# Second block: two prefetched weight units split behind the norm's rows, and another pace of expert loads

## The chip, the cores and the metric

The kernel runs on one core of one Trainium2 chip. The metric is the device time of one execution in microseconds (us); the kernel before has a median of 1340.48 us over 3 runs (1337.61 to 1340.64). A core has a matrix engine (PE, with its weight loads PEld), a vector engine (DVE), a scalar engine (ACT), GpSimd (POOL) and a sync engine (SP). In this kernel SP's queue issues all transfers from HBM that are named below.

## The reference, cut to what matters

The program is two layers of a first block (gated attention, a gated linear attention and a spatial gating unit, merged and normalised) and then a second block with a router and 32 experts. Here is where the change lies: the end of the first block's last layer, and the second block.

```python
out = merge(y_attn, y_gla, y_sgu, m_a, m_g, m_s)            # m @ w_out
x = layer_norm(ALPHA * x + gate * out, post_g, post_b)      # 256 rows of 1024
# second block
z = rmsnorm(x, mix_norm) @ w_in_2           # 2568 columns: q, k, v, forget, gate, recurrent input
att = forgetting_attention(q, k, v, log_f)
lru_out = rg_lru(conv(rec_in)) * gelu(gate_in)
x = x + concat([att, lru_out]) @ w_out_2
h2 = rmsnorm(x, ffn_norm)
y = experts(h2)                             # each token's two experts; w_gate, w_up, w_down: 3 MB an expert
out = rmsnorm(x + y, final_norm)
```

## The kernel before, in words

All matrix products of the dense parts are made of float32 values split in two: a weight *unit* (512 rows of 256 columns, 512 KB) is loaded into a tile `raw`, ACT copies it to a rounded high part (`split`, line 97), DVE subtracts that to a low part (line 98), and PE makes three products (high by high, high by low, low by high). The function `unit` issues the load on SP and the split behind it. The tiles `raw` rotate among three buffers, so the load of a unit waits until the split of the third unit before it is done.

`out_proj` (line 1040) is the last product of the first block. In the last layer it takes its 1024 columns in three steps: 512 columns (four units), 256 and 256 (two units each). After each step DVE scales the product by the gate (`ot`, line 1057), adds it to `x` (line 1058) and takes statistics (`bnst`, line 1060). Then `layer_norm` normalises both row tiles, and `make_hT` (line 493) turns the rows: PE transposes (`trh`), ACT and DVE write the high rows `h2Th` and the modulated rows `hmod`, and DVE subtracts them to the low rows `h2Tl` (line 516). The last ACT and DVE instructions of that stand in `self.last_h`.

Four units of `w_in_2` (its recurrent columns) are prefetched during `out_proj`. They are written into tiles named `ew`, which lie where the first block's rows lay; below they are E0 to E3. `self.pending` is a list of functions, and `tick(n)` calls the next n of them: two after the first step of `out_proj`, one after each of the others. Once the rows are there, the product `p2ps` (lines 1214 and 247) takes E0 and E1, and then E2 and E3. Meanwhile POOL and DVE apply the norm's weights to one row tile each (`x<-x,post`, lines 1198 and 1199), ACT squares the rows (line 1201), and a small product `rmps` (line 1208) spreads the two inverse norms over the partitions.

`second_dense` (line 1333) then projects: the forget columns `f` (two units), the gate columns `g` (four), `q` (four), `k` (four) and `v` (four wide units), 18 units in all. It computes the recurrence (`lru`) beside them. Then come the router's small loads (`router_setup`), the attention over two row tiles, and the output product with eight units of `w_out_2`.

The experts' weights are loaded ahead, in slots of 1 MB, by `load_step` (line 114): each call loads the next half of an expert's gate and up weights (`gu`) or its down weights (`dn`). Ten slots are open from the second block's start, three more once the recurrence's tiles are closed (line 1389), five after the dense part, and four in the experts' part. `paced_load` (line 190) counts the units of the whole program and calls `load_step` behind each second one, if there are slots. Up to the second block 162 units are counted. Behind `v` six calls of `load_step` stand together (line 1392); one without a free slot does nothing.

The order of the instructions on each engine's queue is set by a planner, which simulates a timeline and takes the instructions that it holds to be ready, those that are traced earlier first. `issue_after(ins)` puts what is traced under it behind `ins`, where both are on one engine. Each queue is then run in order on the chip.

Of the kernel before, what the change touches and what calls it, by code (L numbers as in the profile page):

```python
# [75 lines left out]
class Builder:  # L76
    def __init__(self, ctx, tc, a):
        self.ctx, self.tc, self.nc, self.a = ctx, tc, tc.nc, a
        self.after, self.last_tr = (), []
        self.n_split, self.share, self.n_lo = 0, 0, 0  # L80
        self.pending = []
        self.n_unit, self.n_load, self.loaded, self.expert_pools = 0, 0, {}, []
        self.ids, self.last_dn = {}, []
        self.n_bank, self.alternate, self.early = 0, False, {}
        self.nraw, self.nhi = 3, 3
# [104 lines left out]
    def paced_load(self, dma):  # L190

        self.n_unit += 1
        if self.expert_pools and self.n_unit % 2 == 0:
            with self.tc.issue_after(dma.ins):
                self.load_step()

# [871 lines left out]
    def first_block(self):  # L1068
        nc, tc, a = self.nc, self.tc, self.a
        with ExitStack() as st:  # L1070
# [92 lines left out]
            with ExitStack() as layer:  # L1163
                self.slot = self.pool("slot1", bufs=2, stack=layer, reuse_waits="tile")
                self.nhalf = 4
                self.layer_pools(layer)
                m2 = self.second_modulation()
                self.lru_const = self.second_setup(lruc)
                self.branches(((0, 256), (256, 512)))
                with ExitStack() as inner:  # L1170
                    self.merge_pools(inner)
                    h2p = self.pool("h2T", side="right", stack=self.right, reuse_waits="tile")
                    self.h2T = [h2p.tile([128, 8, 256], F32R, name=n) for n in ("h2Th", "h2Tl")]
                    pv = self.post_norm(0)
                    for t in range(2):
                        nc.gpsimd.tensor_tensor(x2[:, t], x2[:, t], pv[:, 0], op=OP.mult)
                        nc.gpsimd.tensor_tensor(x2[:, t], x2[:, t], pv[:, 1], op=OP.add)
                    pv = self.post_norm(1)
                    side = self.pool("lru", side="right", stack=self.right, reuse_waits="tile")
                    self.merge(iter(()))  # L1180

                    early = []

                    def early_unit(u):
                        if u % 2 == 0:
                            t = hp.tile([128, 4, 4, 256], F32R, tag="hTh" if u < 2 else "hTl", name="ew")
                            early.extend([(t[:, 0], t[:, 1]), (t[:, 2], t[:, 3])])
                        c0 = 2056 + 256 * (u // 2)
                        self.unit(a["w_in_2"][0][512 * (u % 2):512 * (u % 2) + 512, c0:c0 + 256], 256, early[u])

                    self.pending.extend([lambda u=u: early_unit(u) for u in range(4)])
                    self.out_proj([x2[:, 0], x2[:, 1]], self.gates(), ((0, 1),),
                                  lambda tts: self.make_hT([x2[:, 0], x2[:, 1]], tts, *m2, dst=self.h2T))
                    junk = self.mg.tile([128, D], F32, tag="gate", bufs=2, name="junk")
                    for tt in range(2):
                        eng = nc.vector if tt else nc.gpsimd
                        with tc.issue_after(self.last_h[1]):
                            eng.tensor_tensor(x2[:, tt], x2[:, tt], pv[:, 0], op=OP.mult)
                            eng.tensor_tensor(x2[:, tt], x2[:, tt], pv[:, 1], op=OP.add)
                        ms = self.sm.tile([128, 1], F32, tag="rms", name="rms")  # L1200
                        nc.scalar.activation(junk, x2[:, tt], AF.Square, scale=1.0 / 32, accum_out=ms)
                        self.rsqrt(self.rs2[:, tt:tt + 1], ms)
                    self.hTh, self.hTl = self.h2T

                    R = self.R = side.tile([128, 256], F32, name="rms2")
                    ps = self.psc.tile([128, 512], F32, tag="sc", name="rmps")
                    for tt in range(2):
                        nc.tensor.matmul(ps[:, tt * 128:tt * 128 + 128], self.rs2[:, tt:tt + 1].to_broadcast([128, 128]),
                                         self.ident, start=True, stop=True, skip_group_check=True)
                    nc.scalar.activation(R, ps[:, :256], AF.Copy)  # L1210
                    rT = self.rT = side.tile([128, 4, 259], F32, name="r2T")
                    nc.gpsimd.memset(rT[:, :, 0:3], 0.0)
                    for c in range(2):
                        for j, ps in enumerate(self.gemm_T(early[2 * c:2 * c + 2], 0, 256, "p2ps")):
                            nc.scalar.activation(rT[:, 2 * c + j, 3:259], ps, AF.Copy)
                    for c in range(4):
                        nc.vector.tensor_tensor(rT[:, c, 3:259], rT[:, c, 3:259], R, op=OP.mult)
# [115 lines left out]
    def second_dense(self, st):  # L1333
# [31 lines left out]
        u = self.chunk(w, 1536, 128)  # L1365
# [25 lines left out]
        self.hTr = big.tile([128, 8, 2, 128], F32, name="hTr")  # L1391
        for _ in range(6):
            self.load_step()

        yh[0], yl[0] = (big.tile([128, 4, 256], F32R, tag="ya", bufs=2, name="ya" + n) for n in "hl")
        for tt in range(2):
# [618 lines left out]
```

## Time and profile before

| what | value |
|---|---|
| median of 3 runs | 1340.48 us |
| profiled execution | 1342.97 us |
| its span, first to last instruction | 1341.1 us |
| PE busy | 1253.8 us (93%) |
| DVE busy | 716.0 us (53%) |
| ACT busy | 578.4 us (43%) |
| POOL busy | 350.6 us (26%) |
| mean granted PE clock, as a share of full speed | 0.976 |
| read from HBM | 241.27 MB |

The profile is of one execution, whose own time is 2.49 us over the median. Times in rows are microseconds from the span's start. A busy PE is not PE at its peak, since the ends of matmuls are modelled; how densely they start tells more.

### The profile page before, as it was taken

What the parts mean: (1) busy time and instruction counts of PE and PEld (TensorE: products, weight loads), DVE (VectorE), ACT (ScalarE), POOL (GpSimd) and SP (SyncE); (2) the same over time, 40 slices, a digit from 0 to 9 for tenths busy, and PEclk for the clock granted to TensorE, in tenths of its full rate; (3) what the DMA queues carried; (4) which work ended last, traced back from release to release, by engine and by line L of the source; (5) the groups of instructions that cost most, each with busy time, mean ns of one, the idle gap of its engine ahead of it and who ended that gap; (6) DMA issues with size and microseconds to landing.
All of it is one profiled execution on the core that took longest, in us unless ns stands there. A gap on an engine that the chain in (4) does not pass through costs nothing. (4 is left out here: it accounts for less than half of the span.)

```text
span 1341.1 us, 21494 instructions
## 1 busy us (share of the span) xinstructions
PE 1253.8 (93%) x8099; PEld 934.1 (70%) x8099; DVE 716.0 (53%) x1412; ACT 578.4 (43%) x1099; POOL 350.6 (26%) x373
## 2 busy tenths in 40 slices
PE   5999999999999999999999989999799989999975
PEld 3679778777777666789887878799698685333221
DVE  2546585675553223368778777655787555111102
ACT  2463453535433222346776554544466434222201
POOL 2327743630000101143367455001054020000000
PEclk8999999999999999999999999999899989999988
DMA  9523232211114577545555435246469556999994
GB/s 309 187 64 100 78 90 69 64 47 54 58 48 120 182 240 229 175 157 157 160 165 156 136 96 188 79 118 179 145 243 331 167 200 256 410 409 408 409 409 180
DMA packets 169873, 243.81 MB, mean 182 GB/s; under 512 B 15285, under 2 KB 130205, under 8 KB 169761
## 3 DMA queue, kind: packets, MB, share of 16 engines
q1 hardware_dynamic: 169760, 242.35, 53.7%
q8 instruction: 66, 1.08, 0.3%
q14 instruction: 47, 0.38, 0.1%
HBM read 241.27 MB, written 1.05 MB: 181 GB/s over the span
## 5 line engine op out<-in xcount | busy, mean ns | idle before, releaser
L98 DVE TENSOR_TENSOR wlo<-raw,whi 128x1024 fp32r<-128x1024 f32 (+1 forms) x202 | 251.6, 1250 | 153.0 <-ACT whi L97 151.4
L97 ACT ACTIVATE whi<-raw 128x1024 fp32r<-128x1024 f32 (+1 forms) x216 | 212.6, 993 | 197.5 <-PE mgps L248 35.1
L247 PE MATMUL mgps<-hTh,whi 128*128 128x512 f32 (+1 forms) x384 | 133.6, 349 | 4.9 <-DVE msum L991 2.6
L249 PE MATMUL mgps<-hTh,wlo 128*128 128x512 f32 (+1 forms) x384 | 132.0, 347 | 0.1
L248 PE MATMUL mgps<-hTl,whi 128*128 128x512 f32 (+1 forms) x384 | 131.7, 343 | 0.0
L994 POOL TENSOR_TENSOR msum<-msum,tanh 128x512 f32<-128x512 f32 (+1 forms) x32 | 35.2, 1104 | 343.6 <-DVE tanh L993 325.9
L1781 PE MATMUL gups<-gu,xw 128*64 128x512 f32 (+1 forms) x512 | 100.2, 618 | 6.4 <-DMA gu<-w_up 6.4
L247 PEld LDWEIGHTS mgps<-hTh,whi 128*128 128x128 f32 x384 | 73.4, 192 | 19.6 <-issue 6.2
L249 PEld LDWEIGHTS mgps<-hTh,wlo 128*128 128x128 f32 x384 | 73.3, 191 | 11.7 <-issue 3.6
L248 PEld LDWEIGHTS mgps<-hTl,whi 128*128 128x128 f32 x384 | 73.6, 192 | 9.0 <-issue 1.9
L1781 PEld LDWEIGHTS gups<-gu,xw 128*64 128x64 f32 (+1 forms) x512 | 25.3, 124 | 60.7 <-issue 58.9
L298 PE MATMUL gmt<-whi,hTh 128*128 128x512 f32 x160 | 61.2, 398 | 2.6 <-ACT qs L639 1.3
L299 PE MATMUL gmt<-wlo,hTh 128*128 128x512 f32 x160 | 62.8, 393 | 0.3 <-DVE wlo L98 0.2
L222 POOL TENSOR_TENSOR frs<-rsq,mhalf 128x1 f32<-128x1 f32 x2 | 1.1, 547 | 235.3 <-DVE frs L1955 235.3
L300 PE MATMUL gmt<-whi,hTl 128*128 128x512 f32 x160 | 62.5, 391 | 0.0
L1813 DVE SCALAR_TENSOR_TENSOR eth<-eth,gups 128x256 f32<-128x256 f32 x12 | 5.1, 421 | 102.3 <-ACT eth L1812 102.3
L1836 PE MATMUL dnps<-dn,hm 128*64 128x512 f32 (+1 forms) x256 | 51.4, 610 | 5.1 <-DMA dn<-w_down 5.1
L651 DVE TENSOR_REDUCE ast<-asc 128x1 f32<-128x512 f32 (+1 forms) x48 | 28.6, 600 | 42.2 <-PE asc L646 42.1
L661 ACT ACTIVATE pt<-trp 128x512 f32<-128x512 f32 (+1 forms) x48 | 24.9, 526 | 56.2 <-PE trp L659 50.7
L283 PE MATMUL gmt<-wlo,hTh 128*128 128x256 f32 x160 | 45.7, 286 | 1.8 <-DVE wlo L98 1.8
L98 DVE TENSOR_TENSOR ol<-dnps,oh 128x512 fp32r<-128x512 f32 x24 | 16.6, 690 | 57.2 <-ACT oh L97 57.2
L282 PE MATMUL gmt<-whi,hTh 128*128 128x256 f32 x160 | 45.4, 284 | 0.6 <-ACT g L742 0.6
(571 smaller groups left out, 3282.4 us busy)
## 6 DMA issues: line engine op xcount, KB each, us to landing
raw<-w_in SPq DMA_DIRECT2D x132, 512.0 KB
gu<-w_gate SPq DMA_DIRECT2D x64, 512.0 KB
gu<-w_up SPq DMA_DIRECT2D x64, 512.0 KB
dn<-w_down SPq DMA_DIRECT2D x28, 1024.0 KB
adar<-w_ada SPq DMA_DIRECT2D x32, 512.0 KB
raw<-w_out SPq DMA_DIRECT2D x32, 512.0 KB
adaw<-w_ada SPq DMA_DIRECT2D x16, 512.0 KB
raw<-w_in SPq DMA_DIRECT2D x32, 256.0 KB
```

What stands on the lines that cost most here:

```text
L97: nc.scalar.activation(hi, x, AF.Copy)
L98: return (eng or nc.vector).tensor_tensor(lo, x, hi.bitcast(F32), op=OP.subtract).ins
L247: nc.tensor.matmul(ps, wh, xh, start=(u == 0 and k == 0), stop=False)
L248: nc.tensor.matmul(ps, wh, xl, start=False, stop=False)
L249: nc.tensor.matmul(ps, wl, xh, start=False, stop=(u == len(acts) - 1 and k == 3))
L282: nc.tensor.matmul(out[tt], xh, hi[:, j, :n], start=first, stop=False, skip_group_check=True)
L283: nc.tensor.matmul(out[tt], xh, lo[:, j, :n], start=False, stop=False, skip_group_check=True)
L298: nc.tensor.matmul(out[tt], xh, hi[:, j], start=(i == 0 and j == 0), stop=False)
L299: nc.tensor.matmul(out[tt], xh, lo[:, j], start=False, stop=False)
L300: nc.tensor.matmul(out[tt], xl, hi[:, j], start=False, stop=(i == 3 and j == 1))
L1781: mm = nc.tensor.matmul(u["ps"][pr], u["x"][:, k, pr], u["gu"][ei][k // 4][:, :, k % 4], start=(k == 0), stop=(k == 7), skip_group_check=T ...
L1836: mm = nc.tensor.matmul(ps[pr], hm[:, f, pr], dns[ei][:, f, 512 * hf:512 * hf + 512], start=(f == 0), stop=(f == 1), skip_group_check=True ...
```

## The change: what it does

Of the four prefetched units only E0 and E1 are left in `pending`, so `out_proj` calls both after its first step. E2 and E3 are called after `out_proj`, with `self.after` set to `last_h`: their splits stand behind the last ACT and the last DVE instruction of the norm's rows. Their loads are traced there too, behind the last units of `out_proj`.

The count in `paced_load` is compared with a new `pace`, which is 3, so that an expert's load follows each third unit; behind the six calls it becomes 1, so that each of the eight units of `w_out_2` calls for a load.

```diff
@@ __init__
+        self.pace = 3
@@ paced_load
-        if self.expert_pools and self.n_unit % 2 == 0:
+        if self.expert_pools and self.n_unit % self.pace == 0:
             with self.tc.issue_after(dma.ins):
                 self.load_step()
@@ first_block
-                    self.pending.extend([lambda u=u: early_unit(u) for u in range(4)])
+                    self.pending.extend([lambda u=u: early_unit(u) for u in range(2)])
                     self.out_proj([x2[:, 0], x2[:, 1]], self.gates(), ((0, 1),),
                                   lambda tts: self.make_hT([x2[:, 0], x2[:, 1]], tts, *m2, dst=self.h2T))
+
+                    self.after = self.last_h
+                    for u in (2, 3):
+                        early_unit(u)
+                    self.after = ()
@@ second_dense
         for _ in range(6):
             self.load_step()
+        self.pace = 1
```

## Rows read from the trace of the kernel before

**Rows 1.** Busy us by stretch: from, to, length, engines (instructions), clock, DMA.

```profile
core 0: us, PE busy (x) PEld busy (x) DVE busy (x) ACT busy (x) POOL busy (x), PEclk, DMA share, GB/s
947.50:960.50 13.00, 12.08 (x97) 11.50 (x95) 10.50 (x17) 5.31 (x5) 0.00 (x0) 1.00 0.75 226
...
966.10:985.20 19.10, 16.89 (x112) 15.93 (x112) 14.31 (x21) 9.46 (x17) 5.79 (x3) 0.81 0.15 45
985.20:1021.40 36.20, 36.13 (x286) 35.14 (x286) 30.09 (x47) 26.21 (x42) 16.14 (x9) 1.00 0.99 353
1021.40:1030.90 9.50, 7.48 (x50) 7.33 (x49) 5.91 (x6) 5.20 (x7) 6.13 (x3) 0.82 0.70 261
1030.90:1074.00 43.10, 41.08 (x240) 30.41 (x239) 26.54 (x53) 22.02 (x56) 3.64 (x4) 1.00 0.68 213
...
1130.00:1310.00 180.00, 166.50 (x840) 56.21 (x836) 31.08 (x86) 37.23 (x105) 0.00 (x0) 0.97 1.03 408
```

**Rows 2.** SP's queue during `out_proj`: start, time, line, transfer, count.

```profile
945.05 0.37 SPq L109 DMA_DIRECT2D raw<-w_in  x1
947.67 2.65 SPq L109 DMA_DIRECT2D raw<-w_out  x2
952.28 2.23 SPq L109 DMA_DIRECT2D raw<-w_in  x4
```

**Rows 3.** ACT at the end of `out_proj`; brackets: idle before, and what ended it.

```profile
958.16 1.06 ACT L97 ACTIVATE ew<-raw 128x1024 fp32r<-128x1024 f32 x1 [2.73 <-DMA raw<-w_in]
```

**Rows 4.** DVE at the end of `out_proj`, three of its rows.

```profile
956.61 0.75 DVE L1057 TENSOR_TENSOR ot<-gmt,gate 128x256 f32<-128x256 f32 x2
959.25 1.23 DVE L98 TENSOR_TENSOR ew<-raw,ew 128x1024 fp32r<-128x1024 f32 x1 [1.89 <-ACT ew L97]
...
963.96 0.26 DVE L934 BATCH_NORM_AGGREGATE bnmv<-bnst 128x2 f32<-128x24 f32 x1
```

**Rows 5.** PE: a gap in the last step of `out_proj`, and the first transposes.

```profile
954.70 0.39 PE L283 MATMUL gmt<-wlo,mm 128*128 128x256 f32 x1 [0.87 <-DVE wlo L98]
...
966.13 1.97 PE L505 MATMUL trh<-ident,x 128*128 128x128 f32 x8 [5.65 <-ACT x L942]
```

**Rows 6.** DVE behind the norm's rows.

```profile
976.38 0.69 DVE L516 TENSOR_TENSOR h2Tl<-hmod,h2Th 128x512 fp32r<-128x512 f32 x1
977.00 3.42 DVE L1198 TENSOR_TENSOR x<-x,post 128x1024 f32<-128x1024 f32 x1
...
982.96 1.21 DVE L1199 TENSOR_TENSOR x<-x,post 128x1024 f32<-128x1024 f32 x1
```

**Rows 7.** POOL beside the norm's rows.

```profile
974.02 2.41 POOL L1198 TENSOR_TENSOR x<-x,post 128x1024 f32<-128x1024 f32 x1 [8.88 <-issue]
976.51 2.83 POOL L1199 TENSOR_TENSOR x<-x,post 128x1024 f32<-128x1024 f32 x1
```

**Rows 8.** PE: the last prefetched product, the norms, and a later pause.

```profile
984.20 0.28 PE L249 MATMUL p2ps<-h2Th,ew 128*128 128x256 f32 x1
985.23 0.49 PE L1208 MATMUL rmps<-ident,rs 128*128 128x128 f32 x2 [0.75 <-POOL rs L222]
...
1023.44 0.39 PE L247 MATMUL p2ps<-h2Th,whi 128*128 128x256 f32 x1 [2.02 <-ACT qk2T L1330]
```

**Rows 9.** SP's queue ahead of the attention.

```profile
1026.40 1.18 SPq L133 DMA_DIRECT2D dn<-w_down  x2
1030.70 6.79 SPq L109 DMA_DIRECT2D raw<-w_out  x2
```

**Rows 10.** ACT: the first split of a unit of `w_out_2`.

```profile
1040.15 1.06 ACT L97 ACTIVATE whi<-raw 128x1024 fp32r<-128x1024 f32 x1 [0.44 <-DMA raw<-w_out]
```

**Rows 11.** PE: that unit's first product, and the transpose of two loaded rows.

```profile
1046.81 0.39 PE L282 MATMUL gmt<-whi,y2h 128*128 128x256 f32 x1
...
1049.84 0.23 PE L1531 MATMUL trf<-ident,fnrow 16*128 16x16 f32 x1
```

**Rows 12.** POOL: a copy that waits for one of the router's small loads.

```profile
1048.86 0.30 POOL L1524 CAST before<-braw 128x128 fp32r<-128x128 f32 x1 [13.52 <-DMA braw<-k_f]
```

## The prediction

> **What bounds the kernel now.** I read the busy times by stretch first, then the queues of each engine around the norm, then those ahead of the attention.
>
> Busy times by stretch [rows 1]: from 1130 to 1310 us the transfers are full (share 1.03, 408 GB/s). That is the experts' part, and it ends when the remaining bytes have come. Its slots come free when the dense part and the router are done, so a microsecond won or lost ahead of it moves the end by one. From 985.2 to 1074 the bound is PE: 36.13 of 36.2 us, with 286 matmuls, which is 0.126 us each, and later 41.08 of 43.1. The transfers are full as well up to 1021 (0.99), but PE does not wait for them. Two stretches in between are not full. In 966.1 to 985.2 PE starts only 112 matmuls, at a mean clock of 0.81, and in 1021.4 to 1030.9 only 50, at 0.82: the clock is partly at its lower level (1.2 instead of 2.4 GHz) after pauses of 5.65 and 2.02 us [rows 5, 8].
>
> The pause of 5.65 us is the norm's. PE ends the last step of `out_proj` at 966.13 - 5.65 = 960.48 and starts the transposes at 966.13 [rows 5]. In between DVE is the late one: it idles 1.89 us, does E3's subtraction (1.23 us, from 959.25), and has the statistics of both row tiles behind that, up to 963.96 + 0.26 = 964.22 [rows 4]. It idles for E3's copy on ACT, which waited 2.73 us for E3's load [rows 3]. That load was issued at 952.28, when E2's split had given its buffer back [rows 2].
>
> **First part: E2 and E3 behind the rows.** What goes from DVE ahead of the statistics is 1.89 us of idle time and two subtractions of about 1.2 us [rows 4], 4.3 us. Not all of it is won, as PE is next. E2's load at 945.05 took a buffer that the first unit of `out_proj`'s last step gets now; it can be issued there instead of at 947.67 [rows 2], 2.6 us sooner, and the gap of 0.87 us in which PE waited for its split [rows 5] goes. So PE ends at 959.6. Behind it DVE has three small instructions of the second row tile (0.75 / 2 = 0.38 us each [rows 4]) and the aggregate of 0.26: 961.0 instead of 964.22, 3.2 us sooner. The inverse norm, the normalisation and the transposes follow as before, so the last `h2Tl` ends at 973.9 instead of 977.07, and POOL starts its pair, which waits for the last transposes, at 970.8 instead of 974.02 [rows 6, 7].
>
> What comes back: on ACT two copies of 1.06 us [rows 3] behind its last row. ACT is busy for 9.46 of 19.1 us there [rows 1], and that hides them; without this cover they would cost their 2.1 us in front of the copies out of the product's bank. On DVE two subtractions, 2.4 us, behind the last `h2Tl`. Queued behind them are `x` (L1198 and L1199), whose end lets ACT square the rows, and then the inverse norm, for which PE waits with `rmps` at 985.23, 0.75 us idle [rows 6, 8]. In the order of before this chain gains 3.2 - 2.4 = 0.8 us. If the planner puts L1199 further ahead (before, it stands some 2.5 us behind the end of L1198, at 980.42), up to 3.2. I see no way below nothing: the two subtractions are the same ones that stood ahead of the norm.
>
> PE does not spoil this. The second half of the prefetched product, 48 matmuls, takes 48 x 0.126 = 6.0 us from E2's low part on. If that is done at 973.9 + 1.2 = 975.1, the product ends at 981.1; if it stands behind POOL first, as L1198 did, 2.3 us later, at 983.4. Before it ended at 984.20 + 0.28 = 984.48 [rows 8], so it gains 1.1 to 3.4 us, the same range. I take 2.0 us for this part, midway between 0.8 and 3.2, since the planner's order is in no row.
>
> L1198 on DVE took 3.42 us and L1199, of the same shape, 1.21. POOL's second instruction ran until 976.51 + 2.83 = 979.34, and L1198 ended 1.08 us behind that [rows 6, 7]: it stood still meanwhile. The Trainium skill (SBUF — State Buffer, "Who interferes with whom") says that a DVE instruction with two inputs in SBUF and a GpSimd instruction that reads SBUF hold a shared port for a whole instruction, and the other is blocked. By it the moved subtractions fall into POOL's pair, and the work of both engines adds up whoever is first: this part would be worth the 0.8. If the two engines ran side by side there, it would be worth some 3.1.
>
> **Second part: the pace of the loads.** Of the 18 units of the second block's projections nine were followed by a load, and six are now, since 162 units are counted ahead of them. They stand behind the 3rd, 6th, 9th, 12th, 15th and 18th. So 3 MB less run beside the projections up to about 1026 us. That is worth nothing by itself, since PE is full there [rows 1]: shorter landings make room only where nobody waits. Its worth has two bounds: nothing, and the whole of the later pause, which is 9.5 - 50 x 0.126 = 3.2 us with the time at the lower clock [rows 1, 8]. That pause ended with a copy on ACT and not with a load, so I take nothing.
>
> The three loads come back behind `v`. Before, two `dn` loads stood there at 1026.40 [rows 9]; now the one behind the 18th unit and four of the six calls follow each other, and with the load behind the 15th unit ahead of the pause, the net is 2 MB more in front of the first unit of `w_out_2`, issued at 1030.70 [rows 9]. At 408 GB/s [rows 1] these take 5.1 us. That unit's copy on ACT started at 1040.15, ended by its load [rows 10]; now 1045.3, less the 2.0 us won, 1043.3. With 1.06 and 1.23 us for its split it is ready at 1045.6. PE wants it at 1046.81 - 2.0 = 1044.8 [rows 11]: 0.8 us late. The router's small loads stand behind it in the queue. One landed at 1048.86 [rows 12], and PE transposes a later one at 1049.84 [rows 11], so at most 1.0 us of room is left there. SP itself is not late: the issue of five loads takes some 4 us, and it waits for a buffer until 1030.70 anyway. I take 0.5 us for this part, since DVE and ACT have idle time ahead of that split, with bounds of 0 and 5.1. The load after the first unit of `w_out_2` is one of three that need the later slots and costs nothing: from 1030.9 to 1074 the transfers are busy for 0.68 [rows 1].
>
> **The sum.** -2.0 + 0.5 = -1.5 us. The profiled execution took 1342.97 us (span 1341.1), so it would take 1341.5; the median of the runs is 2.5 us below it, and I expect 1340.48 - 1.5 = 1339.0 us.
>
> **The rivals.** (1) Faster: the norm's 3.2 us all arrive, and the lighter transfers let the planner order ACT so that the pause at 1021.4 goes, 3.2 more: 1334.1. For it speaks that the pause is one of order on ACT and that both stretches get other neighbours; against it, that nothing in the change touches the recurrence on which ACT waits.
> (2) Slower: the loads massed behind `v` decide, at the first product of `w_out_2` and the small rows behind it. From about 2.3 us of lateness that nothing covers PE stands still as at 1021.4, and the clock falls: 5.1 us, and 9.5 - 6.3 - 2.0 = 1.2 for the lower clock, less the 2.0 won, is +4.3: 1344.8. For it speaks the room of 1.0 us at most; against it, ACT's and DVE's idle time.
> (3) The change does not do what it says: the planner moves other splits or the expert loads into the places left, and the norm starts no sooner. Then 1340.5.
>
> **How the numbers follow.** Forecast 0.45, faster rival 0.32, slower rival 0.17, the third 0.06. A measurement of this kernel can tell about 0.3% from no change, that is 4.0 us: below 1336.5 and above 1344.5. So faster 0.33, within 0.50 (the forecast and the third, less 0.01), slower 0.17. The range reaches from 1332.5 to 1346.0: both rivals' times, each with about half of the runs' own spread of 3.0 us. The forecast's own range is 1336.5 to 1341.5.
>
> **What would show it.** Right: the first transposes at about 962.9 and the last `h2Tl` at 973.9; two `ew` subtractions behind it on DVE, one of them long; `rmps` at about 983.2; six `gu` loads up to 1026 us and four in a row behind `v`; PE as full as before up to 1074. Wrong: a pause of PE over 2 us before the products of `w_out_2` or the transpose of the small rows (the slower rival), no pause at 1021 (the faster one), or a norm that starts no sooner.

## The result, and the profile after

The change makes the kernel slower. Nine runs of it have a median of 1346.88 us (1343.95 to 1356.47), beside 1338.82 us for the kernel before in the same rounds; the medians lie 8.1 us apart, and the ratio of the runs is 1.0073 (95% interval 1.0055 to 1.0092), which is 9.8 us. The forecast was 1339.0 us, with a range up to 1346.0.

The two profiled executions differ by 7.06 us (1350.03 to 1342.97). They are not in step when the change begins. The first product of `out_proj` stands here in the order of time of PE's instructions, before and after (start, time, engine, line, instruction, count, idle time before it and what ended it); the last of the rows are the first of the router's products behind the dense part.

```profile
936.49 0.40 PE L298 MATMUL gmt<-whi,mm 128*128 128x512 f32 x1
...
1099.85 0.39 PE L1584 MATMUL rkps<-sel,before 128*128 128x32 f32 x1 [1.17 <-DVE sel L1576]
```

After, PE's rows that answer to [rows 5, 8, 11]:

```profile
932.34 0.40 PE L299 MATMUL gmt<-whi,mm 128*128 128x512 f32 x1
...
958.52 1.97 PE L506 MATMUL trh<-ident,x 128*128 128x128 f32 x8 [3.15 <-ACT x L943]
...
978.17 0.49 PE L1214 MATMUL rmps<-ident,rs 128*128 128x128 f32 x2
...
1012.23 0.39 PE L248 MATMUL p2ps<-h2Th,whi 128*128 128x256 f32 x1 [0.71 <-ACT qk2T L1336]
...
1041.63 0.58 PE L283 MATMUL gmt<-whi,y2h 128*128 128x256 f32 x1 [3.48 <-ACT whi L98]
...
1051.18 0.23 PE L1538 MATMUL trf<-ident,fnrow 16*128 16x16 f32 x1 [2.31 <-DMA fnrow<-final_norm]
...
1053.79 0.44 PE L1433 MATMUL trp<-ident,p 128*128 128x128 f32 x2 [0.59 <-ACT norms L1540]
...
1106.93 0.28 PE L1591 MATMUL rkps<-sel,before 128*128 128x32 f32 x1 [2.17 <-DVE sel L1583]
```

PE comes to `out_proj` at 932.34 instead of 936.49, through work that the change does not touch. So I count from that product. The first transposes stand 26.18 us behind it (before 29.64), `rmps` 45.83 (before 48.74): the norm gained 2.9 us. From `rmps` to the first `rkps` it is 128.76 us, and before 114.62: 14.1 us are lost there. Behind `rkps` nothing changes any more: 241.3 us to the end of the span in both. The sum is 11.2 us, less the 4.15 us of the early start 7.1, which is what the two executions differ by. From here on the distance from `rmps` to `rkps` is the measure of the stretch that went wrong.

The busy times by stretch answer to [rows 1]; the last two stretches lie inside the one from 1030.90.

```profile
core 0: us, PE busy (x) PEld busy (x) DVE busy (x) ACT busy (x) POOL busy (x), PEclk, DMA share, GB/s
...
1012.00:1021.40 9.40, 9.17 (x71) 8.67 (x72) 9.40 (x10) 4.40 (x7) 3.22 (x3) 1.00 0.71 245
...
1030.90:1074.00 43.10, 35.34 (x143) 24.31 (x142) 19.70 (x43) 15.19 (x44) 0.29 (x1) 0.72 0.64 201
...
1038.20:1046.40 8.20, 4.08 (x17) 3.80 (x18) 4.73 (x7) 3.17 (x3) 0.00 (x0) 0.59 0.89 194
...
1056.70:1073.75 17.05, 16.52 (x50) 9.55 (x49) 8.22 (x20) 4.58 (x16) 0.00 (x0) 0.50 0.37 132
```

The pause that stood at 1021 before [rows 8] is smaller: the wait for the same copy on ACT (`qk2T`) now ends at 1012.23 and is 0.71 us instead of 2.02, at the full clock. From 1030.90 on PE starts 143 matmuls in the time in which it started 240 before, and the clock is 0.72 instead of 1.00. It falls twice, each time behind pauses of PE: in the stretch with the pause of 3.48 us, and behind those of 2.31 and 0.59 us, where it then stays at the lower level (0.50) for 17 us although PE is busy for 16.52 of them.

What the lower level costs can be read from a group of the attention's products (`s`) that PE repeats: the first of each group stands 0.94 us behind the one before it at the full clock, and 1.66 us in the last stretch.

```profile
1054.76 0.38 PE L1414 MATMUL s<-c2T,negid 128*128 128x256 f32 x1 [0.17 <-ACT p L1426]
...
1055.70 0.38 PE L1414 MATMUL s<-c2T,negid 128*128 128x256 f32 x1
...
1066.17 0.58 PE L1414 MATMUL s<-c2T,negid 128*128 128x256 f32 x1
...
1067.83 0.58 PE L1414 MATMUL s<-c2T,negid 128*128 128x256 f32 x1
```

By these spacings the work of the 16.52 us would have taken 9.4 us at the full clock. So my estimate of what the lower level costs in this stretch alone is 7 us.

ACT's rows there (as [rows 10]):

```profile
1040.52 1.06 ACT L98 ACTIVATE whi<-raw 128x1024 fp32r<-128x1024 f32 x1 [4.35 <-DMA raw<-w_out]
...
1052.61 1.06 ACT L98 ACTIVATE whi<-raw 128x1024 fp32r<-128x1024 f32 x1 [8.03 <-DMA raw<-w_out]
1053.58 0.16 ACT L1540 ACTIVATE norms<-trf 128x16 f32<-128x16 f32 x1
1053.64 0.38 ACT L1434 ACTIVATE pt<-trp 128x256 f32<-128x256 f32 x1
```

and SP's queue (as [rows 9]; what the second column gives is the time of the issues, not of the transfers; between the `gu<-w_gate` stand the issues of `gu<-w_up`):

```profile
1020.77 0.46 SPq L149 DMA_DIRECT2D gu<-w_gate  x1
...
1021.75 0.43 SPq L149 DMA_DIRECT2D gu<-w_gate  x1
...
1022.94 0.79 SPq L149 DMA_DIRECT2D gu<-w_gate  x1
...
1024.49 1.96 SPq L134 DMA_DIRECT2D dn<-w_down  x2
1027.46 8.22 SPq L110 DMA_DIRECT2D raw<-w_out  x3
...
1037.44 7.64 SPq L1525 DMA_DIRECT2D wr<-w_inner  x4
...
1047.06 0.29 SPq L1536 DMA_DIRECT2D fnrow<-final_norm  x1
1047.45 10.33 SPq L110 DMA_DIRECT2D raw<-w_out  x5
```

The first unit of `w_out_2` comes to ACT 62.35 us behind `rmps`, and before 54.92; the transpose of `fnrow` stands 73.0 us behind it, and before 64.6. ACT has four splits of that weight ahead of `norms` and the attention's first `pt`, where it had two before: the one of [rows 10] and the one here, of ACT's rows before. The fourth waits 8.03 us for a load that SP issued at 1047.45, behind all ten small loads.

```profile
1045.92 1.05 ACT L97 ACTIVATE whi<-raw 128x1024 fp32r<-128x1024 f32 x1
...
1050.11 0.18 ACT L1533 ACTIVATE norms<-trf 128x16 f32<-128x16 f32 x1 [2.56 <-PE trf L1531]
```

The two rows are late because SP comes to their issue late. It issues the second 68.9 us behind `rmps`, and before 60.1; PE's wait for it ends 3.8 us behind that issue. One unit of `w_out_2` more stands ahead of the small loads (three instead of two), and the issues themselves take longer: the third unit's took 3.58 us, from 1032.10 on, and the four of `wr<-w_inner` 7.64 us instead of 4.15. SP's queue before:

```profile
1039.14 4.15 SPq L1518 DMA_DIRECT2D wr<-w_inner  x4
...
1045.28 0.29 SPq L1529 DMA_DIRECT2D fnrow<-final_norm  x1
```

### The profile page after: what moved, and what is told of

It reads as the page before. It is cut to its first block, busy times and chain, and to the rows that moved or that the text cites. A ratio compares the mean times of both kernels' runs of the same rounds, so it can differ in the third digit from the quotient of the medians.

```text
span 1348.2 us, 21495 instructions
## 1 busy us (share of the span) xinstructions
PE 1259.3 (93%) x8099; PEld 936.1 (69%) x8099; DVE 718.6 (53%) x1412; ACT 577.9 (43%) x1099; POOL 345.7 (26%) x373
## 5 line engine op out<-in xcount | busy, mean ns | idle before, releaser
L995 POOL TENSOR_TENSOR msum<-msum,tanh 128x512 f32<-128x512 f32 (+1 forms) x32 | 35.3, 1109 | 341.5 <-DVE tanh L994 323.7
```

## Experiments

Theory A, from these rows: the new pace puts three more loads (3 MB) in a row in front of the units of `w_out_2` and of the small rows; both come late, PE and ACT take their instructions in a fixed order and stand, and the clock falls. Its rivals: the norm part is the loss (B); only the rows' lateness counts (R), only ACT's order (O), only the first units and the clock (W).

All ratios are to runs of the kernel before on the same chip (their medians lay between 1336.9 and 1338.8 us), with 95% intervals; a ratio is not that of the two medians, and can differ from it by 0.2%. The last column is of each profiled execution.

| kernel | median us | ratio | `rmps` to `rkps`, us |
|---|---|---|---|
| before | 1338.82 | 1 | 114.6 |
| after | 1346.88 | 1.0073 (1.0055 to 1.0092) | 128.8 |
| e1: norm part only | 1334.84 | 0.9986 (0.9959 to 1.0013) | 113.4 |
| e2: pace only | 1354.75 | 1.0139 (1.0101 to 1.0176) | 126.1 |
| e3: loads spread | 1349.04 | 1.0076 (1.0051 to 1.0101) | 128.3 |
| e4: ACT's order | 1345.76 | 1.0061 (1.0036 to 1.0086) | 127.7 |
| e8: rows first | 1341.81 | 1.0030 (1.0012 to 1.0048) | 121.2 |
| e9: rows first, ACT's order | 1341.64 | 1.0029 (1.0011 to 1.0047) | 120.2 |
| e10: rows first, loads spread | 1339.77 | 1.0011 (0.9992 to 1.0030) | 120.9 |
| e5: rows early | 1329.90 | 0.9936 (0.9912 to 0.9961) | 110.8 |
| e11: rows and `wr` early | 1331.14 | 0.9941 (0.9920 to 0.9961) | 110.5 |
| e6: norm part, rows early | 1331.47 | 0.9955 (0.9936 to 0.9975) | 111.1 |
| e7: before, rows early | 1335.04 | 0.9974 (0.9957 to 0.9992) | 113.2 |

**The two parts apart.** e1 is the changed kernel with the old pace:

```diff
-        self.pace = 3
+        self.pace = 2
...
-        self.pace = 1
+        self.pace = 2
```

> The changed kernel with the experts' loads at the old pace (one behind each second weight unit throughout), so that of the change only the two prefetched units behind the norm's rows are left. Theory A (the pace is the whole loss: the loads massed behind v make what stands behind them late, and the norm part is a gain that is kept): faster than before by what v's product gained on the start of out_proj, 3.2 us, so about 1335.6 where before is 1338.8 (ratio 0.9976, 0.996 to 0.999); first product of v 3 us earlier against the start of out_proj, first copy of the attention's pt 3 us earlier too. Rival B (the norm part is the loss: an earlier norm shifts the planner's order behind it): slower than before by 5 to 10 us, 1344 to 1349.

e2 is the kernel before with `self.pace = 3`, and 1 behind `v`.

> The kernel before with the new pace of the experts' loads alone (none of the norm part). Theory A (the pace is the whole loss, the norm part gains 3 us and keeps it): slower than the changed kernel by the missing 3 us, so 1348 to 1352 where before is 1337 to 1339; from the matmul of rmps to the first of rkps 128 us as in the changed kernel (before 114.6). Rival B' (the pace costs only together with the earlier norm): 1338 to 1343.

The loss goes with the pace. e1 is not slower (0.9986, which by itself cannot be told from no change). PE comes to the transpose of `fnrow` without a wait, 63.2 us behind `rmps`, as two `dn` and two units stand ahead of the small loads in SP's queue:

```profile
1018.29 1.18 SPq L134 DMA_DIRECT2D dn<-w_down  x2
1021.22 6.04 SPq L110 DMA_DIRECT2D raw<-w_out  x2
...
1036.84 0.29 SPq L1536 DMA_DIRECT2D fnrow<-final_norm  x1
```

e2 loses without the norm part: 126.1 us from `rmps` to `rkps`, and `fnrow` late again. B falls, and so does B'. Its ratio, 18.6 us, is some 7 us worse than these 11.5 us say. Its profiled execution (1348.50 us) is the fastest of its four runs; the others took 1353.93 to 1359.21 us, and where they lost more stays open.

**ACT's order alone.** e4 issues the splits from the fourth unit on behind the second copy of `pt` (one line of the edit):

```diff
-            units = [self.unit(w[512 * u:512 * u + 512, cs]) for u in (1, 0)]
+            units = [self.unit(w[512 * u:512 * u + 512, cs], after=(second,) if 2 * c + 1 - u > 2 else ()) for u in (1, 0)]
```

> The changed kernel, its loads untouched, with the splits of w_out_2 from the fourth unit on issued behind the second copy of the attention's pt, so that ACT comes to the attention's norms, pt and p without waiting for the fourth unit. Rival O (ACT's order is the loss): back to 1335 to 1338, first copy of pt 7 us or more earlier against v. Theory A and rival R (data late: in the changed kernel the transpose of fnrow came at 1051.18 us, and ACT's split that waited 8.03 us began at 1052.61 us, so the order adds at most some 2 us to what the rows hold anyway): 1345 to 1347, the pause of 3.5 us before the products of w_out_2 and the late transpose of fnrow both still there.

```profile
1043.41 1.06 ACT L98 ACTIVATE whi<-raw 128x1024 fp32r<-128x1024 f32 x1 [0.44 <-DMA raw<-w_out]
1051.45 0.18 ACT L1540 ACTIVATE norms<-trf 128x16 f32<-128x16 f32 x1 [6.99 <-PE trf L1538]
```

The split of 8 us has left its place, and ACT waits there nearly as long for the transpose of `fnrow`. O falls: about 1 us of 14.

**The loads spread.** e3 leaves one of the six calls behind `v` (`range(6)` becomes `range(1)`), and the others follow the units of `w_out_2`.

> The changed kernel with one of the six loads behind v left there; the other five follow one by one the weight units of w_out_2. The same loads pass before the router's small rows, but the first units of w_out_2 no longer stand behind five of them, and on ACT only two splits of w_out_2 stand ahead of the attention. Rival R (the small rows alone hold the attention: the transpose of fnrow on PE, norms on ACT): rows still late, so still some 5 us slower than before, 1343 to 1346, with the transpose of fnrow as late against v as in the changed kernel (some 25 us behind the first product of v). Rival O (only ACT's order, the fourth split ahead of the attention, costs): loss gone, 1335 to 1338. Theory A (lateness of units and rows together): between, about 1341; the 3.5 us pause before the products of w_out_2 gone.

```profile
1045.42 0.39 PE L283 MATMUL gmt<-whi,y2h 128*128 128x256 f32 x1 [0.87 <-ACT whi L98]
...
1054.21 0.28 PE L1538 MATMUL trf<-ident,fnrow 16*128 16x16 f32 x1 [4.55 <-DMA fnrow<-final_norm]
```

The pause of 3.5 us ahead of the products is gone, and the one ahead of `fnrow` has grown from 2.31 to 4.55. The same loads stand ahead of the rows, which are as late against `rmps` as after the change (73.2 us). I had expected 1341 by theory A. R had the lateness of the rows right and not the size: it said 1343 to 1346, and 1349.04 came. W alone falls, as the pause that it names is gone and the loss is not.

**The rows first.** e8 moves the two loads of `fnrow` from the last to the first place of the router's ten small loads (and takes them out of the last); e9 adds e4's edit, e10 adds e3's.

```diff
         rc = self.rc = self.pool("rc", side="right", stack=self.right, reuse_waits="tile")
+        rows = rc.tile([16, 128], F32, name="fnrow")
+        nc.sync.dma_start(rows[0:8], a["ffn_norm_2"][0].rearrange("(k p) -> k p", p=128))
+        nc.sync.dma_start(rows[8:16], a["final_norm_2"].rearrange("(k p) -> k p", p=128))
         self.places = rc.tile([128, 512], F32, name="places")
```

> The changed kernel with one thing changed in the order of the router's ten small loads: the two of fnrow go first instead of last, some 10 us earlier on SP. All the experts' loads and three units of w_out_2 still pass in front of them. ACT still has the split of the fourth unit (queued behind the other small loads) ahead of the second copy of pt. Rival R (only the rows' lateness counts): first copy of pt some 10 us earlier, the time back to 1334 to 1338. Theory RO (rows and, once these are in time, ACT's order: the next wait on ACT is the split of the fourth unit, which ended an 8 us wait at 1052.61): first copy of pt 8 to 10 us earlier, but the second still at 1053 to 1055, so that of 9 us lost 3 to 5 come back, 1341 to 1344.

> The same order of the small loads (fnrow first), and beside it the splits of w_out_2 from the fourth on issued behind the second copy of the attention's pt. Theory RO: both waits gone, the loss gone and the gain of the norm part seen, 1332 to 1337, from rmps to rkps 111 to 115 us. Rival R: like the run with the row first alone. Rival W (the late first units of w_out_2, and the clock that falls in the pause before their products, cost most): 1341 to 1346.

> The changed kernel with both partial repairs: one load behind v instead of six, the others behind w_out_2's units one by one (this alone gave nothing, 1349.0 us), and fnrow first of the router's small loads (this alone 1341.8 us). Theory A, now in two waits one behind the other (w_out_2's first split late: a pause of 3.5 to 3.8 us on PE and half clock behind it; then the rows late): both are shortened, so 1335 to 1340, from rmps to rkps 115 to 119 us, against 128.8 in the changed kernel, 128.3 with the spread alone, 121.2 with the row first alone. Rival (the bytes ahead of the rows decide alone; spreading the loads moves none of them behind the rows): as with the row first alone, 1341 to 1343, 121 us.

PE of e8:

```profile
1040.64 0.58 PE L283 MATMUL gmt<-whi,y2h 128*128 128x256 f32 x1 [3.77 <-ACT whi L98]
...
1046.47 0.28 PE L1538 MATMUL trf<-ident,fnrow 16*128 16x16 f32 x1
```

The wait for `fnrow` is gone, and 7.6 of the 14.1 us come back. The first `pt` comes only 4.5 us earlier against `rmps` (70.9 instead of 75.5), not 8 to 10: the products of `w_out_2` that stand ahead of the transpose on PE wait for their unit as before, and run at the lower clock. The planner has also put the fourth split behind `norms` here; e4 showed what that alone is worth, about 1 us. The busy times of e8 (columns as above) tell how the 7.6 us come back: the second stretch at the lower level is not there.

```profile
1036.40:1047.90 11.50, 7.05 (x31) 6.31 (x31) 5.20 (x8) 3.85 (x6) 0.00 (x0) 0.55 0.76 164
1047.90:1097.60 49.70, 44.27 (x319) 36.23 (x317) 24.93 (x72) 21.96 (x67) 9.25 (x12) 1.00 0.48 168
```

e9 takes the next split out of the attention's way and wins 1 us at most: the step that I had added to R, ACT's order as the second wait, falls again. Its time is also in W's range. e10 takes the pause of 3.77 us away, and `rmps` to `rkps` does not get shorter (120.9), as the rival had said; its time of 1339.77 us lies in theory A's range all the same, with a ratio that overlaps e8's. Its rows show why the distance stays, PE and then ACT:

```profile
1042.85 0.39 PE L283 MATMUL gmt<-whi,y2h 128*128 128x256 f32 x1 [0.39 <-ACT whi L98]
...
1056.31 0.99 PE L1441 MATMUL a2ps<-pt,v 128*64 128x128 f32 x8 [2.67 <-ACT pt L1434]
```

```profile
1053.44 1.06 ACT L98 ACTIVATE whi<-raw 128x1024 fp32r<-128x1024 f32 x1 [3.85 <-DMA raw<-w_out]
```

PE now stands for a copy of `pt` that is queued behind a later split, and that split waits for a unit behind the router's small loads. Each repair lets PE run up to the next late load.

**The rows early.** e5 loads `fnrow` at the start of the projections, into a tile of another pool that is free then (the later loads go; that part is left out here):

```diff
         neg = cst.tile([128, 8], F32R, name="negid")
+        self.fnrow = rows = self.mcst.tile([16, 128], F32, name="fnrow")
+        nc.sync.dma_start(rows[0:8], a["ffn_norm_2"][0].rearrange("(k p) -> k p", p=128))
+        nc.sync.dma_start(rows[8:16], a["final_norm_2"].rearrange("(k p) -> k p", p=128))
```

> The changed kernel with the small rows of fnrow loaded some 50 us earlier, into memory that is free then, so that their transpose, norms and what hangs on it no longer stand between v and the attention; experts' loads and the units of w_out_2 come in the same order as in the changed kernel. The planner then lets the attention's pt go ahead of the splits of w_out_2 on ACT. Rival R (rows hold the attention): loss gone and the gain of the norm part seen, 1334 to 1338. Theory A: most of the loss gone, 1336 to 1341, what stays being the late units of w_out_2. Rival W (only the late first units of w_out_2 and the clock that falls in that pause count): 1344 to 1347, the pause before the products of w_out_2 unchanged.

e6 is e5 with e1's pace, e7 the kernel before with this edit alone, and e11 is e5 with `wr` early too.

> The norm part of the change, the old pace of the experts' loads, and the rows of fnrow loaded some 50 us earlier. It stands beside the changed kernel with its row early (1329.9 us). Rival R (the pace harms only through the rows that it makes late): the same within 2 us, 1328 to 1332, from rmps to rkps 110 to 112 us. Theory A (late units of w_out_2 cost on their own too): 2 to 4 us faster than with the new pace, 1326 to 1328, from rmps to rkps 107 to 109.

> The kernel before with nothing of the change, only the rows of fnrow loaded some 50 us earlier. It tells what an early row is worth where the rows are not late: in the kernel before PE came to their transpose without a pause (1049.84 us, right behind the products of w_out_2). Theory A/R (the early row takes away the wait that the new pace made, and little else): 0 to 3 us faster than before, from rmps to rkps 112 to 114.6 us. Rival (the early row is worth 10 us or more by itself, whatever the pace): 1325 to 1330.

> The changed kernel with the rows of fnrow and the router's weights (wr, five loads) all loaded some 80 us earlier, so that the units of w_out_2 from the fourth on no longer stand behind the small packets of wr. Beside it stands the changed kernel with the row alone early (1329.9 us), where those packets held the DMA engines busy at 12 to 92 GB/s for about 10 us behind 1036 us. If what stays of the loss there is the lateness of w_out_2's units: 2 to 5 us faster than it, 1325 to 1328. If the attention that goes ahead covers it already, as PE's 30.77 us of 31 from 1031 to 1062 say: the same within 2 us, 1328 to 1332, the loads of the experts only coming earlier.

e5 is faster than both kernels, by 0.64% than the one before, and below the ranges of R and A. With the transpose of `fnrow` done at 970.67, the planner puts the attention directly behind `v`, on PE and ACT. The units of `w_out_2` are as late as after the change, and PE is full, at the full clock (the stretch from 1031 to 1062, columns as above; ACT's first `pt`, 60.5 us behind `rmps` instead of 75.5):

```profile
1031.00:1062.00 31.00, 30.77 (x199) 23.26 (x197) 20.44 (x45) 17.43 (x49) 0.32 (x1) 1.00 0.91 299
```

```profile
1037.96 0.66 ACT L1437 ACTIVATE pt<-trp 128x256 f32<-128x256 f32 x2 [1.83 <-PE trp L1436]
```

So e5 changes two things at once, the rows' landing and the order that follows from it, and is worth more than the 14.1 us that were lost (17.9 us from `rmps` to `rkps`). With the rows early the pace costs nothing: e5 and e6 stand at 110.8 and 111.1, and their ratios overlap. That is what R had said of e6; theory A had said 2 to 4 us for the late units. Nor does the pace gain anything that these runs can tell. e7 has only the early row, where it was not late, and is worth 3.5 us (0.9974). In e11 `wr` is out of the way and the time stays the same (0.9941). But its fourth unit is issued only 2.4 us earlier than e5's (67.7 instead of 70.1 us behind `rmps`), so the run does not tell what much earlier units would be worth.

## Why the prediction was wrong

**What was right.** The norm's part, step by step. Counted from `out_proj`'s start, the transposes come 3.46 us earlier (predicted 3.2). The sum there was the gap of 0.87 us that goes and the shorter pause (3.15 instead of 5.65). The two subtractions stand behind the last `h2Tl`:

```profile
967.63 2.33 DVE L517 TENSOR_TENSOR h2Tl<-hmod,h2Th 128x512 fp32r<-128x512 f32 x1
969.87 1.21 DVE L99 TENSOR_TENSOR ew<-raw,ew 128x1024 fp32r<-128x1024 f32 x1
971.01 1.21 DVE L1204 TENSOR_TENSOR x<-x,post 128x1024 f32<-128x1024 f32 x1
...
972.49 1.15 DVE L99 TENSOR_TENSOR ew<-raw,ew 128x1024 fp32r<-128x1024 f32 x1
```

`rmps` gained 2.9 us, where 2.0 was taken between 0.8 and 3.2. From the first transposes to `rmps` it is 19.65 us, and before 19.10 [rows 5, 8], so that only 0.55 us of the two subtractions came back. I had said that one of them would be long beside POOL; none is. POOL's pair ran from 964.21 to 966.58 and from 966.66 to 969.40, and what stood still were the last two instructions of `h2Tl`: 1.18 us (from 965.96) and the 2.33 us above, where two of them beside an idle POOL took 1.28 together. Both end 0.56 us behind POOL's. That is the same 2.2 us that L1198 lost before (3.42 us instead of 1.21 [rows 6]), at another place. These rows agree with the rule of the Trainium skill (SBUF — State Buffer, "Who interferes with whom") that the prediction weighed. But the 0.8 us that I drew from it did not come, as the stall was there before and after.

Right too: the sign named for the slower rival came (a pause over 2 us ahead of the products of `w_out_2`, and one ahead of the transpose), and of the pause at 1021 nothing was to be won. It did shrink, and with the pace: 0.71 or 0.72 us in the kernels with the new pace, 2.0 to 2.4 in those with the old one. But from `rmps` to the first product of `v` it is 46.0 us in e1 and in e5 alike, so half of the faster rival came without its gain. A microsecond ahead of the experts moved the end by about one: while `rkps` came between 1088 and 1109 us, the way from it to the end of the span was 238.7 to 242.3 us in all thirteen kernels.

**What failed** is the second part's sum: "I take 0.5 us for this part, since DVE and ACT have idle time ahead of that split". It cost 14.1 us from `rmps` to `rkps`, and the bound of 5.1 was too low. Five things in it:

1. The lateness. Five loads in a row were foreseen, and 2 MB net were priced. SP's queue shows the five, three `gu` and two `dn`, behind the last unit of `v`, against two `dn`, so 3 MB more. The unit came to ACT 7.4 us later against `rmps`, not 5.1; 3 MB at 408 GB/s [rows 1] are 7.7 us.
2. "SP itself is not late". It came to the small rows' last issue 8.8 us later against `rmps`, as the issues ahead of them took longer.
3. The idle time of ACT and DVE. It covers nothing when the work that could fill it stands behind the waiting instruction. On ACT it did: `norms`, `pt` and `p` stand behind the splits, and on PE the attention stands behind the transpose of two small rows. I looked at how much idle time there was and not at whose it was.
4. The small rows. I saw that they had 1.0 us of room and are queued behind the units [rows 11, 12], and priced only the first wait. e8 shows theirs at 7.6 us.
5. The clock, priced at 1.2 us in the slower rival, which named the place and the mechanism and was given 0.17. It stood at the lower level in two stretches, one of 17 us. By the estimate above that one costs 7 us, and the first (4.08 us busy) at most 2. The kernel before has such time too (0.82 from 1021.4 to 1030.9), so about half of the 14.1 us is the clock. No run separates it from the waits: in e5, without the pauses, both are gone together.

What explains the loss is thus theory A as two waits one behind the other, with the clock in both. 7.6 us come back with the rows in time (e8); that is hardly more than the second stretch at the lower level costs, which a wait of under 3 us set off. Up to 7.7 us stay (from e8's 121.2 to e1's 113.4), which neither a spread of the loads (e10) nor ACT's order (e9) brings back. That these are the price of the late units of `w_out_2`, behind which the attention stands, is argued from what is left over, and no run shows it alone. Only the rows early, which take the attention out from behind both, bring all of it back.

## What to carry to other kernels

A load that is moved is priced at the smallest thing that stands behind it in its queue: here two rows of 4 KB each, whose transpose PE had to pass, decided over 3 MB of weights that nobody waited for. Before calling a wait covered by idle time, read which instructions stand behind the waiting one on its engine, and whether the cover is among them. Price a pause of PE with the stretch at the lower clock that can follow it: here pauses of 2.31 and 0.59 us were followed by 17 us of it. A small load that the next stage cannot start without belongs to a time with empty queues, and to memory that is free then.

## What the runs showed of the hardware

A small load is as late as its place among the issues of its queue: with the rows' two loads first of ten (e8) PE's wait for them went away, behind the same megabytes. With as many loads ahead of them, only spread (e3), they were as late as after the change (73.2 and 73.0 us behind `rmps`). In both kernels PE's wait ended 3.4 to 3.8 us behind the last row's issue. The Trainium skill (DMA: Bandwidth & Descriptors, "Two DMAs through the same engine are not ordered") says that the descriptors of one queue of an engine start in order, though a later one may complete before an earlier write; the rows fit the first half, though they cannot tell that order from the order of SP's issues, and no run here shows the second.

Small packets hold the queue for longer than their bytes say. With `wr` in the queue (e5, 1034 to 1048 us in 40 slices, mean busy share of the DMA engines in tenths, and what they moved):

```profile
DMA  9999999999999999999999999941220388979100
GB/s 433 433 386 386 421 433 398 389 363 372 380 351 369 342 354 351 342 354 339 354 363 357 275 225 144 110 84 43 20 11 5 22 49 70 55 45 58 8 3 7
DMA packets 7410, 3.33 MB, mean 238 GB/s; under 512 B 5420, under 2 KB 6956, under 8 KB 7409
```

Of 7410 packets 5420 are under 512 B. The four loads of `wr<-w_inner`, 32 KB each, took SP 4.15 us to issue before, 7.64 after the change and 10.27 in e3, where many other issues take some 0.4 us. The loads are the same in all three; what differs is what stands ahead of them in the queue. Near the end of the stretch the engines are 0.7 to 0.9 busy at 45 to 70 GB/s. e11, which has these loads elsewhere, is no faster.
